# Latents turned piece by piece, scale and offset in quarters, split first transfers and a halved last tile in a fused encoder block

## The chip, the cores and the metric

The kernel runs on one core of a Trainium2 chip. The metric is device time in microseconds of one execution. The core has a matrix engine (TensorE, here PE, with the loading of weights shown apart as PEld), a vector engine (VectorE, DVE), a scalar engine (ScalarE, ACT), GpSimd (POOL) and a synchronising engine (SyncE, SP). Each has its own stream of instructions, which runs in order; SP, ACT and POOL also issue the transfers (DMAs) between the main memory and the on-chip memory.

## The reference

One layer of a streaming encoder with 256 tokens, width 2048, everything in float32. The residual stream `h` goes through four blocks, each closed by a LayerNorm over `ALPHA * h + block(h)`:

```python
h = LN(ALPHA*h + 0.5*swiglu_ffn(h, ffn1))             # 2048 -> 2 x 5504 -> 2048
proj = h @ w_in                                       # q, k, v of A; latents of B; gates
y_a = chunked_relbias_attention(qa, ka, va) @ w_o_a   # A: 16 heads of 64, relative bias
c_q  = rms_norm(q_lat, q_a_norm)                      # B: low-rank latents, 512 each
c_kv = rms_norm(c_kv, kv_a_norm)
y_b = mla(c_q @ w_q_b, c_kv @ w_kv_b, k_pe) @ w_o_b   # B: 16 heads of 128 + 64 rotary
h = LN(ALPHA*h + (sig(g_a)*y_a + sig(g_b)*y_b) @ w_out)
h = LN(ALPHA*h + cross_attention(h, LN(mem)))         # 4 heads of 512, 256 memory tokens
h = LN(ALPHA*h + 0.5*swiglu_ffn(h, ffn2))
```

A LayerNorm is `(x - mean) * rsqrt(var + eps) * g + b`, with a scale `g` and an offset `b` for each of the 2048 columns.

## The kernel before

**Numbers in two halves.** Each float32 operand of a large product is split into a rounded half `hi` and the rest `lo` (`split` at lines 234 and 235, `halves` for weights at lines 242 and 245). A product is then three passes: hi by hi, hi by lo, lo by hi. The cast to `hi` runs on ACT, the subtraction that gives `lo` on DVE.

**Weights.** All weights pass once through the core, in pieces of up to 128 x 2048 numbers (1 MB). A piece is fetched by SP into one of three `raw` tiles and split into one of two pairs of `hi` and `lo` tiles; `run` keeps the fetches about two pieces ahead of their use. Some pieces (`Sums`) are combined further on DVE (lines 189 and 191), which saves products.

**PSUM.** Two pools of four banks each, `mm` and `at`. A `pair_group` fills four tiles of 128 x 512 for two column groups and two token tiles; groups alternate between the pools. The attention parts use `at` for scores, transpositions and outputs.

**The order.** The program is a list of items (`add`, `weave`), each a function with the weights that it needs. A planner then orders the instructions of every engine by priority, by place in the list and by its own estimate of when an operand is ready. `prio(SOON)` and `prio(NEAR)` put the instructions of an item forward by 400 and 100 places, `prio(LATE)` puts them back by 400. The order that it finds is fixed; on the chip every engine follows it and waits where something is late.

**The start (`start`).** Twelve warm-up products (line 475) run on PE. Then eight steps `k`, each with two slices of the transposed input `xT` (0.25 MB, issued by ACT at line 483) and 1 MB of weights (SP, line 486; in halves for the first two steps); the slices and the weights are split, and 24 products of 512 columns follow (`mm_pair`, line 299).

**The mixer.** After the gates, the latents' product (`w_lat`) is formed. `lat_scale` normalises the two latents per token; `gb_apply(0)` multiplies the residual stream with the scale of the first LayerNorm and adds its offset, in four quarters of 512 columns: each loads a quarter of `g` and of `b` from POOL into two `w2` tiles (of five that all parts share) and runs two multiplications (line 444) and two additions (line 445) on DVE. Then come the shared rotary key (`kpe`, with swaps by SP at line 891), the query and key projections of the first two A heads (`a_proj(0)`, 64 products in two halves, lines 265 and 267), and `lat_turn`: both latents are transposed on PE (line 877, 16 transpositions of 128 x 128 into four `at` tiles), multiplied by their gains to give `hi` on ACT (line 881), and the rest `lo` on DVE (line 882). The A heads follow in pairs: projections, transpositions of the probabilities (line 774), scores (line 924), outputs (lines 965 and 966). The latents are first used by the rotary queries (line 255), after the A heads' projections. The 16 B heads (`b_scores`, `b_trans`, `b_proj`, `b_out`) come after; the softmax between scores and transposition runs on DVE and ACT (lines 762 to 769, 1039).

**The end.** The last product, `ffn2`'s second half over 19 row tiles, is done in groups of 4, 4, 4, 4 and 3 row tiles (`out_proj`, line 286). For the last 512 columns all groups of the first token tile run first and then those of the second (`skewed`), so that the first tile's LayerNorm and output run beside the second's products. After the last group, `finish` adds the 512 columns to `h` (line 701), takes their statistics (`bn_stats`, line 377), and `final_steps` aggregates them (line 382), forms the inverse root, applies scale and offset (lines 1320 and 1321) and writes the result.

## Time and profile before

| | us |
|---|---|
| median of three runs | 2495.51 (2494.61 to 2496.06) |
| the profiled execution | 2493.65 |
| its span in the profile | 2491.9 |

| engine | busy us | share of the span |
|---|---|---|
| PE | 2471.8 | 99% |
| PEld | 2082.8 | 84% |
| DVE | 2055.1 | 82% |
| ACT | 1332.9 | 53% |
| POOL | 28.8 | 1% |

The transfers move 490.03 MB, 197 GB/s on average. A row of the timeline gives start, duration, engine, line, operation, written tile `<-` read tiles, the shape, and in brackets the idle time of that engine before the row and what ended it. A row of the waits gives the waiting instruction, what it waited for, microseconds in all, times and the longest. In a row such as `x16` several instructions are merged; the duration is of all of them.

### The profile page before, as it was taken

The page shows a single profiled execution, that of the slowest core. Times are in us where ns is not written, and L with a number is a line of the kernel's source. Part 1 is how long each engine was busy: PE and PEld are TensorE (multiplying, and loading weights), DVE is VectorE, ACT ScalarE, POOL GpSimd, SP SyncE. Part 2 cuts the span into 40 slices and gives each one's busy share as a digit, 9 for nine tenths or more (in the row PEclk, how much of TensorE's full clock was granted, in tenths as well). Part 3 has the DMA queues.
Part 4 walks back from the last instruction along what each step waited for, and adds up shares of the span by engine and source line. Part 5 has one row for each costly group of instructions (what it writes and reads, how often), then busy time and mean ns, then how long its engine had stood idle before and what let it go on. Part 6 is the DMA issues. An engine that isn't in the chain of part 4 may idle for free.

```text
span 2491.9 us, 30464 instructions
## 1 busy us (share of the span) xinstructions
PE 2471.8 (99%) x11966; PEld 2082.8 (84%) x11966; DVE 2055.1 (82%) x2313; ACT 1332.9 (53%) x1798; POOL 28.8 (1%) x69
## 2 busy tenths in 40 slices
PE   9999999999999999999999999999999999999998
PEld 7888888889888888899888888898888888888886
DVE  6999889899778988676678798557888988898986
ACT  5555555555455555555445565545555555555552
POOL 0000000000000001000000000000000000000000
PEclk9999999999999999999999999999999999999999
DMA  7655555556645556543466557544555555655664
GB/s 255 240 191 208 188 201 209 203 186 204 236 160 203 210 203 226 199 153 119 168 221 219 186 175 247 189 167 148 205 204 186 203 186 203 210 198 201 206 211 141
DMA packets 72512, 490.03 MB, mean 197 GB/s; under 512 B 8368, under 2 KB 8752, under 8 KB 17200
## 3 DMA queue, kind: packets, MB, share of 16 engines
q1 hardware_dynamic: 66384, 467.11, 53.7%
q0 software_dynamic: 4256, 17.83, 2.2%
q10 hardware_dynamic: 1728, 3.15, 0.4%
q8 instruction: 93, 1.52, 0.2%
q14 instruction: 51, 0.42, 0.0%
HBM read 484.77 MB, written 2.10 MB: 195 GB/s over the span
## 4 chain that ended last, share of the span: by engine, by line
PE 95%; DVE 2%; DMA 1%; ACT 1%; issue 0%; SPq 0%; DVEq 0%; ACTq 0%; POOL 0%
PE mm L299 25%; PE at L299 25%; PE mm L353 10%; PE at L353 10%; PE mm L286 8%; PE mm L265 7%; PE mm L267 4%; PE mm L255 2%; PE at L924 1%; PE at L286 1%; DVE lo L245 1%; PE at L774 1%; DMA H<-xT 0%; PE at L1279 0%; PE at L404 0%; PE at L1255 0%
## 5 line engine op out<-in xcount | busy, mean ns | idle before, releaser
L242 ACT CAST hi<-raw 128x1024 fp32r<-128x1024 f32 (+1 forms) x848 | 801.8, 987 | 604.2 <-PE at L299 182.6
L245 DVE TENSOR_TENSOR lo<-raw,hi 128x2048 fp32r<-128x2048 f32 (+2 forms) x425 | 904.3, 2129 | 239.6 <-ACT hi L242 237.8
L299 PE MATMUL mm<-hi,T 128*128 128x512 f32 (+1 forms) x1280 | 298.4, 383 | 1.4 <-ACT hi L234 1.4
L242 ACT CAST X<-H 128x1024 fp32r<-128x1024 f32 (+1 forms) x162 | 164.9, 1034 | 216.7 <-DVE H L191 86.6
L299 PEld LDWEIGHTS mm<-hi,T 128*128 128x128 f32 x1280 | 238.0, 188 | 46.1 <-ACT hi L234 2.0
L299 PE MATMUL at<-hi,T 128*128 128x512 f32 x1072 | 257.0, 389 | 0.0
L245 DVE TENSOR_TENSOR X<-H,X 128x2048 fp32r<-128x2048 f32 (+1 forms) x81 | 182.3, 2251 | 67.7 <-ACT X L242 67.7
L299 PEld LDWEIGHTS at<-hi,T 128*128 128x128 f32 x1072 | 201.2, 188 | 41.9
L299 PE MATMUL mm<-lo,T 128*128 128x512 f32 (+1 forms) x640 | 153.8, 382 | 0.0
L299 PE MATMUL at<-hi,H 128*128 128x512 f32 x608 | 144.7, 390 | 0.9 <-DVE w L632 0.9
L299 PEld LDWEIGHTS mm<-lo,T 128*128 128x128 f32 x640 | 119.1, 188 | 21.8
L299 PEld LDWEIGHTS at<-hi,H 128*128 128x128 f32 x608 | 113.9, 188 | 24.7 <-DVE w L632 1.3
L299 PE MATMUL at<-lo,T 128*128 128x512 f32 x536 | 132.6, 389 | 0.0
L265 PE MATMUL mm<-T,hi 128*128 128x512 f32 x512 | 124.4, 394 | 0.0
L299 PEld LDWEIGHTS at<-lo,T 128*128 128x128 f32 x536 | 100.6, 188 | 20.9
L299 PE MATMUL mm<-hi,H 128*128 128x512 f32 x480 | 116.1, 392 | 0.0
L191 DVE TENSOR_TENSOR H<-H,raw 128x512 f32<-128x512 f32 (+1 forms) x162 | 109.5, 676 | 1.7
L265 PEld LDWEIGHTS mm<-T,hi 128*128 128x128 f32 x512 | 94.2, 189 | 19.3 <-issue 0.9
L299 PEld LDWEIGHTS mm<-hi,H 128*128 128x128 f32 x480 | 89.3, 188 | 18.2 <-DVE w L274 0.2
L189 DVE TENSOR_TENSOR H<-raw 128x1024 f32<-128x1024 f32 (+1 forms) x81 | 97.1, 1199 | 3.0 <-DMA raw<-ffn_w_in 1.7
L353 PE MATMUL mm<-X,X 128*128 128x512 f32 x348 | 95.9, 392 | 0.0
L242 ACT CAST X<-raw 128x1024 fp32r<-128x1024 f32 (+1 forms) x54 | 55.4, 1035 | 51.5 <-DVE raw L191 31.9
(321 smaller groups left out, 3913.9 us busy)
## 6 DMA issues: line engine op xcount, KB each, us to landing
raw<-ffn_w_in SPq DMA_DIRECT2D x150, 1024.0 KB, 4.8
raw<-ffn_w_out SPq DMA_DIRECT2D x66, 1024.0 KB, 4.8
raw<-w_gate SPq DMA_DIRECT2D x32, 1024.0 KB, 4.8
raw<-ffn_w_out_r SPq DMA_DIRECT2D x16, 1024.0 KB, 4.9
raw<-w_qk SPq DMA_DIRECT2D x16, 1024.0 KB, 4.8
raw<-w_o_b SPq DMA_DIRECT2D x16, 1024.0 KB, 4.8
raw<-w_out SPq DMA_DIRECT2D x16, 1024.0 KB, 4.8
raw<-w_xk SPq DMA_DIRECT2D x16, 1024.0 KB, 4.8
```

Source lines behind the costliest of these rows:

```text
L189: self.nc.vector.tensor_tensor(two[0], two[1], raw[:, :m].unsqueeze(1).to_broadcast([P, 2, m]), ALU.add)
L191: self.nc.vector.tensor_tensor(t[:, a * m:a * m + m], t[:, b * m:b * m + m], raw[:, a * m:a * m + m], ALU.add)
L242: self.nc.scalar.copy(hi[:, c:d], src[:, c:d])
L245: self.nc.vector.tensor_tensor(lo[:, :n], src, hi[:, :n].bitcast(F32), ALU.subtract)
L255: self.nc.tensor.matmul(ps, w[wi][:, cols[j]:cols[j] + P], x.at(xi, kt), start=(j + wi + xi == 0), stop=(j == n - 1 and wi == 1),)
L265: self.nc.tensor.matmul(ps, hi[kt], x.both(kt), start=(kt == 0), stop=False)
L267: self.last_mm = self.nc.tensor.matmul(ps[:, :S], lo[kt], x.at(0, kt), start=False, stop=(kt == n - 1))
L286: self.last_mm = self.nc.tensor.matmul(ps, x.at(xi, kt)[:, tt * P:(tt + 1) * P], w[wi][:, j * 512:(j + 1) * 512], start=(start and j + wi ...
L299: self.last_mm = self.nc.tensor.matmul(ps[tt, g][:, :n], x.at(xi, kt)[:, tt * P:(tt + 1) * P], w[wi][:, c:c + n], start=first and j + wi + ...
L353: self.last_mm = self.nc.tensor.matmul(bank[:, :m], a[xi], v[wi][:, c * m:(c + 1) * m], start=own and first and wi + xi == 0, stop=own and ...
L774: self.nc.tensor.transpose(ps[:, i * P:(i + 1) * P], s[:, c:c + P], self.ident)
L924: nc.tensor.matmul(ps[:, c0:c0 + nk], q[:, tt * P:(tt + 1) * P], k[:, :nk], start=(j == 0), stop=(j == len(parts) - 1))
```

## The change

It has four parts.

- **The latents** are turned in four pieces of four transpositions and one `at` tile each. Two stand behind the two halves of the second pair's projections (`a_proj(1)`), two behind those of the third (`a_proj(2)`), in place of one block behind `a_proj(0)`; their work on ACT and DVE gets the priority `NEAR`.
- **Scale and offset** of the first LayerNorm go in quarters, behind B heads 2, 5, 8 and 11, with the priority `LATE`, in place of all four behind `lat_scale`.
- **The start**: the first step's weights come in quarters and its two slices of x one by one; ACT issues the slices of the first three steps at once and SP those of the others, each two steps ahead of its weights' turn; the rounding of the first step's slices runs on DVE.
- **The end**: for the second token tile of the last 512 columns, the sum of the first four groups is added to `h` early, and the last group of three row tiles is formed as two tiles of 256 columns, each with its own addition and statistics; the last LayerNorm's statistics then have five parts.

```diff
-    def mm_tok(self, ps, tt, w, x, kts, start, stop):
+    def mm_tok(self, ps, tt, w, x, kts, start, stop, c=0, m=512):
...
-                        ps, x.at(xi, kt)[:, tt * P:(tt + 1) * P], w[wi][:, j * 512:(j + 1) * 512],
+                        ps, x.at(xi, kt)[:, tt * P:(tt + 1) * P], w[wi][:, j * 512 + c:j * 512 + c + m],
...
-    def gb_apply(self, i, h):
+    def gb_apply(self, i, h, qs=range(4)):
 
         nc = self.nc
-        for q in range(4):
+        for q in qs:
...
+        v = [xr[k // 4][:, k % 4 * 2:k % 4 * 2 + 2, :] for k in range(KT // 2)]
+
+        def x_load(q, k, step=2):
+            for i in range(0, 2, step):
+                q.dma_start(v[k][:, i:i + step, :], t["xT"][:, 2 * k + i:2 * k + i + step, :])
+        for k in range(3):
+            x_load(nc.scalar, k, 2 if k else 1)
         for k in range(KT // 2):
...
-            nc.scalar.dma_start(v, t["xT"][:, 2 * k:2 * k + 2, :])
-            for c in range(0, 2048, 1024 if k < 2 else 2048):
-                d = c + (1024 if k < 2 else 2048)
-                nc.sync.dma_start(raw[:, c:d], src[:, c:d])
-            self.split(v, xT.blk(0, 2 * k, 2), xT.blk(1, 2 * k, 2))
+            n = (512, 1024, 2048)[min(k, 2)]
+            for c in range(0, 2048, n):
+                nc.sync.dma_start(raw[:, c:c + n], src[:, c:c + n])
+            if 2 < k + 2 < KT // 2:
+                x_load(nc.sync, k + 2)
+            for i in range(0, 2, 1 if k == 0 else 2):
+                m = 1 if k == 0 else 2
+                hi, lo = (xT.blk(a, 2 * k + i, m) for a in (0, 1))
+                if k == 0:
+                    nc.vector.tensor_copy(hi, v[k][:, i:i + m, :])
+                    nc.vector.tensor_tensor(lo, v[k][:, i:i + m, :], hi.bitcast(F32), ALU.subtract)
+                else:
+                    self.split(v[k], hi, lo)
...
-                st[tt] = self.ln_begin()
+                st[tt] = self.ln_begin(5 if self.cut and tt else 4)
...
+                if cut and again and i == len(groups) - 1:
+                    for a in range(2):
+                        p = self.mm_tile()
+                        self.mm_tok(p[:, :S], 1, w, x(), grp, True, True, a * S, S)
+                        hs = h[1][:, n * 512 + a * S:n * 512 + a * S + S]
+                        with self.prio(SOON):
+                            nc.vector.tensor_tensor(hs, hs, p[:, :S], ALU.add)
+                            nc.vector.bn_stats(st[1][:, 3 + a, :], hs)
+                    return
                 for tt in tts:
...
+                    short = cut and again and i == len(groups) - 2
+                    self.mm_tok(ps[tt], tt, w, x(), grp, i == 0, short or i == len(groups) - 1)
+                    if short:
+                        hs = h[tt][:, n * 512:(n + 1) * 512]
+                        nc.vector.tensor_tensor(hs, hs, ps[tt], ALU.add)
...
-        def lat_turn():
-            self.c = self.act(["X0", "X1"])
-            for k in range(2):
-                for b in range(2):
-                    ps = self.at_tile()
+        def lat_turn(k, b):
+            def fn():
+                if k + b == 0:
+                    self.c = self.act(["X0", "X1"])
+                ps = self.at_tile()
+                for i in range(2):
...
+                    with self.prio(NEAR):
                         nc.scalar.mul(hi, p, gain)
                         nc.vector.scalar_tensor_tensor(lo, p, gain, hi.bitcast(F32), ALU.mult, ALU.subtract)
+            return fn
...
-        self.add(lambda: self.gb_apply(0, self.h), prio=LATE)
...
-        def a_proj(i):
+        def a_proj(i, side=()):
...
             for k in range(2):
                 self.add(one(k), t["w_qk"][i, k])
+                for f in side[k:k + 1]:
+                    self.add(f)
...
         a_proj(0)
-        self.add(lat_turn)
...
-                a_proj(i + 1)
+                a_proj(i + 1, [lat_turn(i, b) for b in range(2)] if i < 2 else ())
...
+            if h in (2, 5, 8, 11):
+                self.add(lambda q=h // 3: self.gb_apply(0, self.h, (q,)), held=int(h % 2 == 0), prio=LATE)
```

More of the change, by code (lines that the diff above doesn't have):

```diff
@@ L111, in __init__ @@
         self.chain = None
+        self.cut = False
     def name(self, s):
@@ L370, in rsqrt, with ln_begin @@
                 nc.vector.scalar_tensor_tensor(y, a, 1.5, y, ALU.add, ALU.mult)
[L373 to L374 removed]
+    def ln_begin(self, n=4):
+        return self.small.tile([P, 5, 6], F32, tag="bn", name=self.name("bn"))[:, :n, :]
     def ln_piece(self, st, h, n):
@@ L545, in ffn @@
                 self.add(late)
+                self.add(lambda: setattr(self, "cut", True))
             def out(hid=hid):
@@ L552, in out @@
                 if end:
-                    self.out_proj(tag + "_w_out_r", nf, x, False, st, steps, tags, 2)
+                    self.out_proj(tag + "_w_out_r", nf, x, False, st, steps, tags, 2, cut=tags is None)
                 else:
@@ L703, in finish, with out_proj @@
             if n == 0:
-                st[tt] = self.ln_begin()
+                st[tt] = self.ln_begin(5 if self.cut and tt else 4)
             self.ln_piece(st[tt], h[tt], n)
-    def out_proj(self, wname, nk, x, scale, st, steps=None, tags=None, n0=0, other=False):
+    def out_proj(self, wname, nk, x, scale, st, steps=None, tags=None, n0=0, other=False, cut=False):
         nc, t, h = self.nc, self.t, self.h
```

17 lines of the change are left out of this document (6 added, 11 removed).

## The prediction

> **What bounds the kernel now.** I read the page first, then the waits of the matmul engine, then the timelines of the places that the change touches.
>
> ```profile
> span 2491.9 us, 30464 instructions
> PE 2471.8 (99%) x11966; PEld 2082.8 (84%) x11966; DVE 2055.1 (82%) x2313; ACT 1332.9 (53%) x1798; POOL 28.8 (1%) x69
> PE 95%; DVE 2%; DMA 1%; ACT 1%; issue 0%; SPq 0%; DVEq 0%; ACTq 0%; POOL 0%
> ```
>
> TensorE (PE) is busy for 2471.8 of 2491.9 us and carries 95% of the chain that ended last. The change takes away no matmul, so all it can win lies in the 20.1 us in which PE stood still, plus stretches where PE ran slowly. The waits of PE say where these are; the rest, some 12 us, is the tail after the last matmul, and comes last below:
>
> ```profile
> PE at L877 <- DVE X L882: 3.6, 1, 3.6
> PE mm L299 <- ACT hi L234: 1.4, 2, 0.8
> PE at L475 <- DVE w L451: 1.1, 1, 1.1
> PE at L299 <- DVE w L632: 0.9, 1, 0.9
> PE at L404 <- DVE h L396: 0.5, 2, 0.3
> ```
>
> L877 is the turning of the latents, L299 with L234 the first group at the start. L632 and L404 are in code that the change leaves alone.
>
> **The turning of the latents (L877).** The timeline of all engines around the wait, and two stretches of the table by windows (length; busy time of PE, PEld, DVE, ACT, POOL; granted clock; DMA share; GB/s):
>
> ```profile
> 955.97 0.69 DVE L444 TENSOR_TENSOR h<-h,w 128x512 f32<-128x512 f32 x1 [1.84 <-DMA w<-gb]
> 958.38 2.08 PE L267 MATMUL mm<-T,lo 128*128 128x256 f32 x16
> 965.86 1.04 PE L877 MATMUL at<-ident,H 128*128 128x128 f32 x8
> 966.65 2.76 PE L265 MATMUL mm<-T,hi 128*128 128x512 f32 x11
> 967.12 2.29 DVE L245 TENSOR_TENSOR lo<-raw,hi 128x2048 fp32r<-128x2048 f32 x1
> 969.32 0.69 DVE L445 TENSOR_TENSOR h<-h,w 128x512 f32<-128x512 f32 x1
> 969.93 2.28 DVE L245 TENSOR_TENSOR lo<-raw,hi 128x2048 fp32r<-128x2048 f32 x1
> 972.46 2.91 DVE L882 SCALAR_TENSOR_TENSOR X<-at,vecs,X 128x256 fp32r<-128x256 f32 x7
> 972.99 0.44 PE L877 MATMUL at<-ident,H 128*128 128x128 f32 x2 [3.58 <-DVE X L882]
> 975.76 2.96 PE L267 MATMUL mm<-T,lo 128*128 128x256 f32 x16
> 965.86:984.21 18.35, 14.77 (x82) 12.79 (x80) 16.54 (x25) 8.04 (x15) 0.00 (x0) 0.91 0.50 171
> 1004.42:1009.99 5.57, 5.57 (x34) 4.92 (x33) 2.62 (x2) 2.27 (x4) 0.34 (x2) 1.00 0.37 104
> ```
>
> All sixteen transpositions of the turning are issued together. PE does eight of them, into two PSUM tiles, starts the next projection (L265), and then cannot go on: the eight others go out in twos, each pair behind an L882, which empties half a tile on VectorE (DVE). DVE has two splits of 2.29 us and an addition of the LayerNorm offset (L445) ahead of the first L882, 5.26 us by their rows.
>
> From 965.86 to 984.21 PE does the 16 transpositions and two halves of a query-key projection. One such half alone takes 5.57 us (last row). Eight transpositions take 966.65 - 965.86 = 0.8 us, so 16 take 1.6; cut into four places they need about 0.1 us more at each, an estimate. That makes 2 x 5.57 + 1.6 + 0.4 = 13.1 us against 18.35: 5.2 us are lost, the wait of 3.58 and 1.6 in which PE runs slowly behind it (the 16 matmuls of L267 take 2.96 us there and 2.08 at 958.38). The granted clock of 0.91 lies in the same stretch.
>
> The change puts one tile between projections, four times, some 5.6 us apart. Its drain (two multiplications on ScalarE, two L882, put forward by the priority) then has a projection's 5.57 us where before it had none. The last piece is the tight one: transpositions and scores follow it at once and ask for tiles within about 1 us. Bounds: a gain of all 5.2 us, or of 2.6 if half of the loss reappears there. I take 5.2, since the same tiles serve the later pairs of heads, five requests in a row, without a wait in the list above. Who needs the latents later? The rotary projections, some 80 us after; a piece that is two projections late costs nothing there.
>
> The Trainium skill, "TensorE: Matmul & The Clock Gate", Part 1, says that an idle window of about 3.4 us brings the clock to half. The trace agrees, with 0.91 over a stretch that holds 3.58 us of idleness. By that rule a wait cut to half would lose no clock either, which makes the second rival below 0.8 us better than I put it.
>
> **The start (L299 with L234).** Rows of the timeline, one of the chain, and two windows:
>
> ```profile
> 1.06 4.78 PE L475 MATMUL at<-w 128*128 128x128 f32 x24 [1.06 <-DVE w L451]
> 5.48 0.62 ACT L234 CAST T<-H 128x512 fp32r<-128x512 f32 x1 [2.79 <-DMA H<-xT]
> 6.67 3.99 PE L299 MATMUL mm<-hi,T 128*128 128x512 f32 x16 [0.83 <-ACT hi L234]
> 7.62 1.14 ACT L234 CAST hi<-raw 128x512 fp32r<-128x512 f32 x2 [0.48 <-DMA raw<-ffn_w_in]
> 13.23 0.62 ACT L234 CAST T<-H 128x512 fp32r<-128x512 f32 x1 [2.99 <-DMA H<-xT]
> 14.85 36.56 PE mm L299 x160
> 0.00:4.00 4.00, 2.94 (x14) 2.94 (x14) 0.17 (x1) 1.49 (x2) 1.69 (x10) 1.00 0.46 131
> 4.00:8.00 4.00, 3.17 (x18) 2.70 (x18) 1.87 (x3) 2.05 (x4) 0.00 (x0) 1.00 1.02 391
> ```
>
> The group has 192 matmuls of 36.56 / 160 = 0.228 us, so 43.9 us. It begins at 6.67 and ends at 14.85 + 36.56 = 51.41. The warm-up matmuls (L475) hold PE until 5.84, so it can't begin earlier; without gaps it would end at 49.7. The upper bound is therefore 1.7 us. The lower bound is set by the transfers, which already run at full rate: 131 GB/s make 0.52 MB by 4.0 us, and 0.39 MB come per us after that. The first weights arrived in halves of 0.5 MB beside 0.25 MB of x; the second half, with 1.5 MB moved by 6.5 us (two slices of x and the megabyte of weights), was seen at 7.62, so a landing is seen about 1.1 us after its bytes. In the new order the first matmul needs 0.13 MB of x and 0.25 MB of weights; with two queues sharing, that is 0.52 MB moved, 4.0 us, seen at 5.1, cast (half of 1.14) by 5.7: PE starts at 5.84. The second quarter needs 1.0 MB, so 5.3 + 1.1 + 0.6 = 7.0, where PE would want it at 6.3; the later quarters and the second block come in time, and the third slice of x, for which ScalarE sat 2.99 us at 13.23, is asked for at once rather than behind casts. So of 1.7 us some 0.5 are lost again: I take a gain of 1.2, bounds 0 and 1.7. That more and smaller transfers cost more on the SP queue I price at nothing: five slices of x now stand between the weight blocks there, 0.25 MB or 0.6 us each at 0.39 MB per us, and later blocks wait for their buffer, not for the queue. Uncovered, that is the 3 us that would undo the gain.
>
> **Scale and offset among the B heads.** Sixteen DVE adds and multiplications and eight POOL transfers leave the stretch from 952 to 990 us and go, a quarter at a time, behind heads 2, 5, 8 and 11. The price of one, the landings of the transfers of the scale (L440), the windows of the B heads, what DVE waited for there, and who waited for the last step of a softmax (L769):
>
> ```profile
> L444 DVE TENSOR_TENSOR h<-h,w x24: 675/684/694, 956.0 to 1824.0; 128x512 f32<-128x512 f32 x24
> DMA to landing us min/median/max: 3.3/4.1/9.9
> 1097.00:1160.00 63.00, 62.93 (x435) 58.46 (x435) 42.63 (x100) 34.49 (x86) 0.00 (x0) 1.00 0.38 132
> DVE sm_r L767 <- ACT w L765: 14.9, 13, 1.5
>   PEld at L774: 0.7, 2
> ```
>
> The 16 instructions are 16 x 0.684 = 10.9 us. DVE has 63.0 - 42.6 = 20.4 us free in this stretch, mostly the holes of about 1.1 us in which a softmax waits for its exponential (14.9 us in 13), and one addition fits such a hole. But PE is full, and two of the 16 softmaxes were finished only as PE came for them (0.7 us, last row): DVE work that slips in ahead delays PE. If every instruction had a chance of 2 in 16 to do so, it would cost 16 x 0.684 / 8 = 1.4 us; as the quarters have the lowest priority, I take half, 0.7. Below: nothing, as PE has no wait there to lose. Above: each quarter standing on the path with its four instructions (2.74 us) and the one wait for a transfer seen, 1.84 us (row of 955.97): 4 x 4.58 = 18.3 us. The space: of five w2 buffers three are in use by softmaxes and two go to a quarter, so nothing is left over, but nothing is short. On POOL's queue the eight transfers leave their place ahead of the A heads' biases, for which PE has no wait above, and come to where POOL is idle (0.00 in the window).
>
> **The tail.** From the timeline, with one row of half the width from elsewhere:
>
> ```profile
> 972.13 0.41 DVE L274 TENSOR_TENSOR w<-w,mm 128x256 f32<-128x256 f32 x1
> 2477.48 0.75 DVE L1321 SCALAR_TENSOR_TENSOR h<-h,y,T 128x512 f32<-128x512 f32 x1
> 2479.48 0.69 DVE L701 TENSOR_TENSOR h<-h,mm 128x512 f32<-128x512 f32 x1 [1.25 <-PE mm L286]
> 2480.20 0.69 DVE L377 BATCH_NORM_STATS2 bn<-h 128x6 f32<-128x512 f32 x1
> 2480.93 0.27 DVE L382 BATCH_NORM_AGGREGATE mv<-bn 128x2 f32<-128x24 f32 x1
> ```
>
> Behind the last matmul stand an addition and a statistic of 512 columns, 2480.93 - 2479.48 = 1.45 us. Halved, only 256 columns stay behind it: 0.41 for the addition and the same, estimated, for the statistic, with gaps about 0.85; gain 0.6. Nine matmuls of 512 columns (2.05 us) become 18 of 256 at 2.08 / 16 = 0.13 (L267 at 958.38), 2.3 us at most, so 0.1 to 0.3 go back. The early addition of 0.69 finds DVE free from 2478.23 on (a hole of 1.25 us), if it isn't ordered ahead of the other half's last steps. I take 0.4; bounds 0 and 0.6.
>
> **The sum.** -5.2 - 1.2 + 0.7 - 0.4 = -6.1 us. The profiled execution took 2493.65 us, 1.86 below the median of the three runs, 2495.51. Against the median I forecast 2489.4, that is -0.24%. What a measurement of this kernel can tell from no change is 0.2%, 5 us: the border lies at 2490.5.
>
> **The rivals.** First, slower: the quarters stand in the way of the B heads. Place: DVE between a head's scores and its transposition, price up to 4.58 us a quarter as above. It speaks for it that PE is full and that the trace has such a wait of 1.84 us; against it that of 24 instructions of L444 one waited. It cancels the other gains (6.8 us) from 1.7 us a quarter on, and decides for slower from 2.95 (11.8 / 4); at full price 2495.5 - 6.8 + 18.3 = 2507.0.
>
> On this the Trainium skill, "SBUF — State Buffer", section "SBUF: two separate sides", speaks against the change: while DVE runs certain instructions, POOL can't write the descriptors of its transfers. The landings of 3.3 to 9.9 us, for transfers of one size, fit that, but no row here shows a lock. As a mechanism of this kernel, in rows, a quarter would come late by one split, 2.29 us, and DVE wait for it: 4 x 2.29 = 9.2 us if all are bare, so 2495.5 - 6.8 + 9.2 = 2497.9, within 0.2% of before; it has a chance of 0.04, since no transfer of the later two such passes was waited for.
>
> Second, the wait of L877 is not gone but moved to the reuse of the last piece's tile: half of the 5.2 us returns, 2492.0, or a like loss arises among the B heads. For it: PE's order is fixed beforehand and DVE is busy 16.54 of 18.35 us there. Against: one tile at a time, and DVE is rid of the scale and offset.
>
> Third, the start isn't sooner because the transfers run at full rate either way: -4.9 us, 2490.6, at the border.
>
> **How the numbers follow.** The forecast has 0.62; the first rival 0.08, the late transfers 0.04, the second 0.14, the third 0.12. Half of the third lies on either side of the border: faster 0.62 + 0.06 = 0.68, same 0.04 + 0.14 + 0.06 = 0.24, slower 0.08. The likeliest alone spans 2486.5 (upper bounds of all gains, 7.5, and the waits at L632 and L404, 1.4, gone by a new order) to 2490.5. The range takes in the second and third rivals with 1.5 us of cost among the heads: 2486.5 to 2493.5.
>
> **What would show it.** The latents: no wait of PE at L877 and a clock of 1.00 from 960 to 1000 us; the first group ending near 50.2; no new wait of PE on L769 or on the scale and offset between 1080 and 1190; the aggregate of the last LayerNorm 1.0 to 1.2 us behind the last matmul. I am wrong if PE waits over 3 us among the B heads, or if the pieces of the latents wait for L882 as before.

## The result and the profile after

| | before | after |
|---|---|---|
| median, us | 2495.42 (2493.59 to 2498.33, 10 runs) | 2487.53 (2486.73 to 2493.1, 10 runs) |
| the profiled execution, us | 2493.65 | 2488.81 |
| its span, us | 2491.9 | 2487.0 |

The ratio is 0.9971, with an interval of 0.9961 to 0.998: 7.9 us or 0.29% faster. The two profiled executions are only 4.84 us apart, since the one of before lies 1.8 us below its median and the one of after 1.3 us above. A second profile of the changed kernel, taken later, has a span of 2484.8 us.

Lines of the code move with the change: 299 becomes 300, 265 and 267 become 266 and 268, 877 and 882 become 905 and 911, 444 and 445 become 445 and 446, 767 and 769 become 795 and 797, 774 becomes 802, 924 becomes 955. In the experiments that add lines further up, L878 and L890 stand for L877, L883 and L895 for L882. First the busy time of the engines, from the page of the changed kernel:

```profile
PE 2470.8 (99%) x11975; PEld 2083.1 (84%) x11975; DVE 2056.5 (83%) x2319; ACT 1332.8 (54%) x1797; POOL 28.7 (1%) x69
```

The busy time of PE is 1.0 us less, the span 4.9 us. Most of what went is idle time. All waits of PE that are listed (total, times, longest):

```profile
PE at L405 <- DVE h L397: 1.1, 2, 0.9
PE at L476 <- DVE w L452: 1.1, 1, 1.1
PE at L300 <- DVE w L647: 1.0, 1, 1.0
PE mm L354 <- DVE H L236: 0.6, 1, 0.6
PE at L802 <- DVE w L797: 0.5, 1, 0.5
```

The wait of the latents (3.6 us at L877 before) and that of the first group (1.4 us) are gone. L802 on L797, the transposition of the probabilities waiting for the last step of a softmax, is new in this list. The waits at L405 and L354, for DVE, are in code that the change leaves alone; they were 0.5 us and none before, and they differ from profile to profile.

The timeline of the changed kernel, by place: a half of a projection without a piece and the next one with the first piece in it (two pairs of transpositions), the scores and ACT's work behind the first pair of the last piece (990.52), the last quarter among the B heads, the tail.

```profile
965.34 3.82 PE L266 MATMUL mm<-T,hi 128*128 128x512 f32 x16
969.00 2.08 PE L268 MATMUL mm<-T,lo 128*128 128x256 f32 x16
970.91 0.38 PE L905 MATMUL at<-ident,H 128*128 128x128 f32 x2
973.97 0.44 PE L905 MATMUL at<-ident,H 128*128 128x128 f32 x2
975.18 2.06 PE L268 MATMUL mm<-T,lo 128*128 128x256 f32 x16
...
991.01 0.48 ACT L910 ACTIVATE X<-at,vecs 128x256 fp32r<-128x256 f32 x1
991.38 0.48 ACT L808 COPY w<-at 128x384 f32<-128x384 f32 x1
991.49 1.35 PE L955 MATMUL at<-w,w 64*128 64x128 f32 x8
...
1174.76 0.68 DVE L446 TENSOR_TENSOR h<-h,w 128x512 f32<-128x512 f32 x1
1176.77 0.33 PE L802 MATMUL at<-ident,w 128*128 128x128 f32 x1 [0.55 <-DVE w L797]
...
2470.16 5.03 PE L287 MATMUL mm<-X,H 128*128 128x512 f32 x30
2475.36 0.40 DVE L749 TENSOR_TENSOR h<-h,mm 128x256 f32<-128x256 f32 x1
2476.25 0.29 DVE L383 BATCH_NORM_AGGREGATE mv<-bn 128x2 f32<-128x30 f32 x1
```

Of the kernel before, the row that ends with its last matmul is this:

```profile
2474.52 4.92 PE L286 MATMUL mm<-X,H 128*128 128x512 f32 x21
```

So the last matmul ends at 2479.44 us before and at 2475.19 after. The aggregate started 1.49 us behind it (2480.93, in the prediction) and now starts 1.06 us behind it (2476.25).

The chain of the changed kernel at its start (start, duration, what):

```profile
1.06 5.49 PE at L476 x24
6.55 43.88 PE mm L300 x192
```

The first group now follows the warm-up products at once and ends at 6.55 + 43.88 = 50.43; before it was 51.41. The warm-up itself ended later in this profile (6.55 us for 5.84), so the group begins only 0.1 us sooner than before (6.67); the rest of the gain is that its 192 products leave no gaps. Two stretches of the table by windows (length; busy PE, PEld, DVE, ACT, POOL; clock; DMA share; GB/s), first before, then after:

```profile
966.00:980.00 14.00, 10.42 (x56) 8.96 (x54) 12.19 (x18) 6.14 (x13) 0.00 (x0) 0.88 0.49 175
```

```profile
966.00:980.00 14.00, 14.00 (x83) 11.48 (x82) 8.38 (x8) 5.78 (x9) 0.00 (x0) 1.00 0.50 180
1097.00:1160.00 63.00, 62.98 (x422) 57.76 (x421) 49.26 (x113) 35.04 (x85) 3.79 (x7) 1.00 0.45 144
```

Between 966 and 980 us PE has no idle time left, the clock is at 1.00, and DVE does 8.4 us of work where it did 12.2. That work is now among the B heads: 49.3 us of DVE in the 63 us where 42.6 stood before. What DVE waited for there:

```profile
DVE sm_r L795 <- ACT w L793: 10.2, 11, 1.4
DVE h L446 <- DMA w<-gb: 0.5, 1, 0.5
```

The holes in which DVE waits for exponentials shrank from 14.9 to 10.2 us: quarters lie in them. One does not: the last quarter's addition at 1174.76 stands just ahead of a softmax's last steps, and PE waits 0.55 us for these at 1176.77.

To put the time to places I took, in each kernel's trace, the start of the first matmul of a stage and the change of its distance from the stage before it (us, against the kernel before). "Latents" is the stretch from the first product of the shared key to the first rotary product, "B heads" from there to the first product behind the heads, which goes out between the last of them; "the end of the second product" is a point inside `ffn2`, near 1900 us. The kernels other than before and after are those of the experiments.

| kernel | end of first group | to LayerNorm 1 | to shared key | latents | B heads | to the end of the second product | to the last matmul | behind it |
|---|---|---|---|---|---|---|---|---|
| after | -1.0 | +0.5 | -0.1 | **-4.5** | +0.5 | +0.5 | -0.1 | -0.7 |
| after, second profile | -1.2 | -0.6 | 0.0 | **-4.6** | +0.3 | -0.3 | 0.0 | -0.7 |
| latents alone | +0.1 | +0.4 | 0.0 | **-0.8** | 0.0 | -0.1 | +1.3 | 0.0 |
| quarters alone | 0.0 | +0.6 | +0.1 | **-5.3** | +0.5 | -0.2 | -0.3 | 0.0 |
| start alone | -1.0 | -0.4 | 0.0 | +0.6 | 0.0 | -0.1 | -0.2 | -0.2 |
| end alone | -0.1 | -0.3 | 0.0 | 0.0 | 0.0 | +0.7 | +1.8 | -0.5 |
| quarters, start, end | -0.8 | -0.5 | 0.0 | **-5.3** | +0.3 | -0.3 | -0.3 | -0.7 |

Stages that no part touches (to LayerNorm 1, to the end of the second product, to the last matmul) vary by up to 1.8 us from profile to profile (+0.5 and +0.5 after come with the waits at L405 and L354 in the list above, +0.7 and +1.8 of the end alone with 2.0 us at L354 in its list), so no stage is read here below half a microsecond unless several kernels agree on it.

### The profile page after: what moved, and what is told of

It reads as the page before. It is cut to its first block, busy times and chain, and to the rows that moved or that the text cites. A ratio compares the mean times of both kernels' runs of the same rounds, so it can differ in the third digit from the quotient of the medians.

```text
span 2487.0 us, 30497 instructions
## 1 busy us (share of the span) xinstructions
PE 2470.8 (99%) x11975; PEld 2083.1 (84%) x11975; DVE 2056.5 (83%) x2319; ACT 1332.8 (54%) x1797; POOL 28.7 (1%) x69
## 3 DMA queue, kind: packets, MB, share of 16 engines
q10 hardware_dynamic: 1152, 1.84, 0.2%
## 4 chain that ended last, share of the span: by engine, by line
PE 96%; DVE 2%; DMA 1%; ACT 1%; issue 0%; DVEq 0%; ACTq 0%
PE mm L300 25%; PE at L300 25%; PE mm L354 10%; PE at L354 10%; PE mm L287 7%; PE mm L266 7%; PE mm L268 4%; PE mm L256 2%; PE at L955 1%; PE at L287 1%; PE at L802 1%; PE at L1311 0%; PE at L1287 0%; PE at L996 0%; DVE lo L246 0%; PE mm L705 0%
## 5 line engine op out<-in xcount | busy, mean ns | idle before, releaser
L354 PE MATMUL mm<-X,X 128*128 128x512 f32 x348 | 95.6, 391 | 0.6 <-DVE H L236 0.6
```

Source lines behind the costliest of these rows:

```text
L354: self.last_mm = self.nc.tensor.matmul(bank[:, :m], a[xi], v[wi][:, c * m:(c + 1) * m], start=own and first and wi + xi == 0, stop=own and ...
```

## Experiments

**The four parts, one at a time.** Each kernel is the one before with one part of the change.

*Latents in pieces alone.*

```diff
-        self.add(lat_turn)
...
-                a_proj(i + 1)
+                a_proj(i + 1, [lat_turn(i, b) for b in range(2)] if i < 2 else ())
```

> The kernel before with the latents alone in four pieces; scale and offset stay behind lat_scale. Theory (the pieces remove the wait at L877 by giving each tile a projection's time): PE no longer waits for L882, PE comes to the rotary projections (L255) 4 to 5 us sooner than in the kernel before, and the time falls by 4 to 5 us, ratio 0.998. Rival (the wait came from DVE being late with the scale and offset, L444 and L445): half of the wait stays or moves, the rotary projections come 1 to 2.5 us sooner at most, ratio 0.999 or more.

2494.94 us beside 2494.7, ratio 1.0 (0.9991 to 1.0008). PE's wait, the window and the timeline of this kernel:

```profile
PE at L877 <- DVE X L883: 3.4, 1, 3.4
966.00:980.00 14.00, 10.62 (x59) 8.64 (x58) 13.93 (x19) 4.34 (x7) 0.00 (x0) 1.00 0.62 215
973.86 1.29 DVE L444 TENSOR_TENSOR h<-h,w 128x512 f32<-128x512 f32 x2
976.27 2.28 DVE L245 TENSOR_TENSOR lo<-raw,hi 128x2048 fp32r<-128x2048 f32 x1
978.47 0.48 DVE L883 SCALAR_TENSOR_TENSOR X<-at,vecs,X 128x256 fp32r<-128x256 f32 x1
979.00 0.44 PE L877 MATMUL at<-ident,H 128*128 128x128 f32 x2 [3.38 <-DVE X L883]
```

The wait is there as before, now at the second pair of the first piece. DVE is full (13.93 of 14 us): the first drain (L883) stands behind multiplications (973.86) and additions of the quarters and a split (976.27). A piece is one tile, and its second pair goes out 0.05 us behind the drain of its first pair (978.47 + 0.48 to 979.00): the second half of a tile waits for the drain of the first half. So the wait lies inside a tile, and one tile at a time does not help when the engine that empties it comes 6 us after the transposition (972.28 to 978.47). Read in this way, the eight transpositions that the block sends at once are the first halves of its four tiles. The theory put first fails. The stage gains 0.8 us in this profile, since the clock stays at 1.00; the medians show no gain.

*Scale and offset in quarters alone.*

```diff
-        self.add(lambda: self.gb_apply(0, self.h), prio=LATE)
...
+            if h in (2, 5, 8, 11):
+                self.add(lambda q=h // 3: self.gb_apply(0, self.h, (q,)), held=int(h % 2 == 0), prio=LATE)
```

> The kernel before with scale and offset alone moved in quarters among the B heads; the latents stay one block behind a_proj(0). Theory: the block still waits for its L882 behind the two splits of 2.29 us on DVE, so PE still waits 2.5 to 3.5 us at L877, the rotary projections come at most 1.5 us sooner; the B heads cost 0 to 1 us; ratio 0.9995 to 1.0005. Rival (DVE was late through the scale and offset): the wait falls under 1 us, the rotary projections come 3 to 5 us sooner, ratio 0.998.

2488.17 us beside 2494.7, ratio 0.997 (0.9959 to 0.9982). The window and the first drains of the latents, which are turned in one block here as before:

```profile
966.00:980.00 14.00, 14.00 (x92) 12.31 (x93) 8.69 (x14) 8.83 (x16) 0.00 (x0) 1.00 0.55 194
969.44 3.37 DVE L882 SCALAR_TENSOR_TENSOR X<-at,vecs,X 128x256 fp32r<-128x256 f32 x8
```

No wait at L877, PE full, the clock at 1.00. The whole gain of the latents, 5.3 us, comes from this part; the rival of the expectation holds.

*The start alone.* The diff of `start` as shown with the change, and nothing else.

```diff
-            for c in range(0, 2048, 1024 if k < 2 else 2048):
...
+            n = (512, 1024, 2048)[min(k, 2)]
...
+            if 2 < k + 2 < KT // 2:
+                x_load(nc.sync, k + 2)
```

> The kernel before with the new first transfers alone. Theory: the first group ends 1.0 us sooner (near 50.4 instead of 51.4 us), all later work of PE is shifted by as much, the time falls by 1 us, ratio 0.9996. Rival (the first microsecond is lost again at the next wait): the first group ends sooner but PE comes to the first LayerNorm's transpositions (L404) at the same time as before, ratio 1.000.

2493.2 us beside 2494.7, ratio 0.9993 (0.9984 to 1.0002). The time alone doesn't tell it from nothing; the first group ends 1.0 us sooner in this trace (50.2 by the stages for 51.2 before), as it does in every kernel that has this part and the twelve warm-up products (0.8 to 1.3 us). The latents' wait is untouched:

```profile
PE at L890 <- DVE X L895: 4.0, 1, 4.0
```

*The end alone.* The diff of `out_proj` as shown with the change.

```diff
+                if cut and again and i == len(groups) - 1:
+                    for a in range(2):
+                        p = self.mm_tile()
...
+                            nc.vector.bn_stats(st[1][:, 3 + a, :], hs)
```

> The kernel before with the last tile halved alone. Theory: PE ends 0.2 us later, the aggregate of the last LayerNorm stands 1.06 us behind PE's end instead of 1.49, and the time falls by 0.2 to 0.4 us, ratio 0.9999, not to be told from 1 by time, only in the profile. Rival (the early addition is ordered ahead of the other half's last steps and delays them): the aggregate comes as late as before or later.

2494.45 us beside 2494.7, ratio 0.9996 (0.9987 to 1.0005). The aggregate starts 1.07 us behind the end of the last matmul, and 1.06 or 1.07 in every kernel with this part, for 1.49 in those without it. The 1.8 us that this profile loses ahead of the last matmul are not in the others; they are waits at L354, which the part does not touch.

Added up, the four medians against before make +0.24 - 6.5 - 1.5 - 0.25 = -8.0 us; the whole change made -7.9. The parts do not help or hinder each other beyond what these runs resolve.

**All but the pieces.** The changed kernel with the latents turned in one block as before; run beside the changed kernel itself.

```diff
-                a_proj(i + 1, [lat_turn(i, b) for b in range(2)] if i < 2 else ())
+                a_proj(i + 1)
...
         a_proj(0)
+        self.add(lat_turn)
```

> The changed kernel with the latents left as one block behind a_proj(0), so quarters, start and tail without the pieces. Theory now (the quarters' move alone takes the wait away, and the pieces cost PE some 0.8 us, since their transpositions go out in twos between other matmuls): no wait at L877, PE comes to the rotary projections about 0.8 us sooner than in the changed kernel, measured from the shared key's product on, and the time is 0.5 to 1 us under the changed kernel's, ratio to the kernel before 0.9967. Rival (the pieces carry a part of the gain in this company): a wait at L877 of over 1 us and a time above the changed kernel's.

> The changed kernel once more beside the others of this call. Both theories: ratio 0.9971 as before, within 0.001; the rotary projections 4 to 5 us sooner than in the kernel before.

Without the pieces 2486.5 us, ratio 0.9967 (0.9955 to 0.9979); the changed kernel beside it 2486.87, ratio 0.9969 (0.9957 to 0.9981). The times are the same; the latents' stretch gains 5.3 us without the pieces and 4.5 to 4.6 with them, in three profiles each. So the pieces cost 0.8 us there.

**Why the quarters were in the way.** They put three things ahead of the first drain: instructions on DVE, DVE's waits for the transfers, and a place in its queue.

*The first quarter stays, the other three move.*

```diff
-        self.add(lambda: self.gb_apply(0, self.h), prio=LATE)
+        self.add(lambda: self.gb_apply(0, self.h, (0,)), prio=LATE)
...
+            if h in (5, 8, 11):
+                self.add(lambda q=h // 3: self.gb_apply(0, self.h, (q,)), held=int(h % 2 == 0), prio=LATE)
```

> The kernel before with the quarters of heads 5, 8 and 11 moved and the first quarter left behind lat_scale; the latents one block. Theory (VectorE's instructions and its wait ahead of L882 add up): four instructions of 0.65 us at spacing and a wait of 1.8 us come back, of which about 3 us fall into holes of VectorE that the quarters-alone run has, so PE waits 0.5 to 2 us at L877. Rival (the wait for the first quarter's transfer alone makes the lateness, which shifts the swaps of the rotary key and all that follows): PE waits 3 us or more, as in the kernel before.

2489.27 us beside 2494.54, ratio 0.9978 (0.997 to 0.9987). PE's wait and two rows of DVE:

```profile
PE at L877 <- DVE X L882: 0.9, 1, 0.9
956.66 0.69 DVE L444 TENSOR_TENSOR h<-h,w 128x512 f32<-128x512 f32 x1 [2.49 <-DMA w<-gb]
969.78 3.37 DVE L882 SCALAR_TENSOR_TENSOR X<-at,vecs,X 128x256 fp32r<-128x256 f32 x8
```

DVE still waits 2.5 us for the first transfer, and PE's wait falls from 3.6 to 0.9 us all the same. That one wait is not the cause by itself.

*The priority put back by 3000 places instead of 400.*

```diff
-        self.add(lambda: self.gb_apply(0, self.h), prio=LATE)
+        self.add(lambda: self.gb_apply(0, self.h), prio=-3000)
```

> The kernel before with one number changed: the priority of scale and offset behind lat_scale is put back by 3000 places instead of 400. Theory (what counts is that VectorE's order has scale and offset ahead of the latents' L882, not where they stand in the list): the wait at L877 falls under 1 us and PE comes from the shared key's product to the rotary projections 3.5 to 5.3 us sooner, ratio 0.997 to 0.9985. Rival (VectorE has not the room for them among the A heads): the wait turns up as waits of PE in the A heads, the same stretch gains under 2 us, ratio 0.999 or more.

2494.55 us beside 2495.14, ratio 1.0 (0.9991 to 1.0009).

```profile
PE at L877 <- DVE X L882: 4.3, 1, 4.3
972.67 2.59 DVE L882 SCALAR_TENSOR_TENSOR X<-at,vecs,X 128x256 fp32r<-128x256 f32 x6
```

The order on DVE stays nearly what it was: the planner gives DVE whatever is ready by its estimate, however low its priority, and on the chip the instruction then stands there. So this run does not show whether DVE would have room for the quarters among the A heads in another order. It shows that priority does not move them, and a place in the list does.

*All sixteen instructions, two transfers instead of eight.*

```diff
-            g, b = self.w2(), self.w2()
-            nc.gpsimd.dma_start(g, self.t["gb"][i, 0:1, cs].to_broadcast([P, 512]))
-            nc.gpsimd.dma_start(b, self.t["gb"][i, 1:2, cs].to_broadcast([P, 512]))
+            if i > 0 or q == 0:
+                g, b = self.w2(), self.w2()
+                nc.gpsimd.dma_start(g, self.t["gb"][i, 0:1, cs].to_broadcast([P, 512]))
+                nc.gpsimd.dma_start(b, self.t["gb"][i, 1:2, cs].to_broadcast([P, 512]))
```

> The kernel before, in which all four quarters of the first LayerNorm use the scale and the offset of the first: two transfers instead of eight, the same sixteen additions and multiplications in the same order on DVE. (The values of three quarters are therefore those of another column; this leaves out six transfers and nothing else.) Open is what of the quarters delays the turning of the latents: their instructions on DVE, or their transfers, which crowd the swap of the shared key (in the kernel before DVE waits 1.7 us for it, with all the quarters moved away not at all). Theory A, the instructions: seven of them still stand ahead of the first L882, the wait of PE at L877 stays at 3.0 us or more and the stretch from the shared key to the first rotary product gains less than 1.0 us. Theory B, the transfers: the swap comes 1.7 us sooner and with it everything behind it in DVE's queue; the wait of PE falls to between 1.5 and 2.3 us, the clock stays at 1.00, and the stretch gains 1.9 + 1.6 = 3.5 us (2.5 to 4.3); time about 2491.5 beside 2495. If the wait falls below 1.0 us, the instructions have no part in it at all.

2492.04 us beside 2495.4, ratio 0.999 (0.9981 to 0.9999). The stages put only 0.3 us of this on the latents, and 1.0 us on the stage ahead of the last matmul, which varies by that much. Its lines are one higher: L445 is the multiplication, L878 the transposition.

```profile
PE at L878 <- DVE X L883: 3.3, 1, 3.3
957.36 0.69 DVE L445 TENSOR_TENSOR h<-h,w 128x512 f32<-128x512 f32 x1 [3.41 <-DMA w<-gb]
972.03 2.90 DVE L883 SCALAR_TENSOR_TENSOR X<-at,vecs,X 128x256 fp32r<-128x256 f32 x7
966.00:980.00 14.00, 10.66 (x56) 9.19 (x55) 12.21 (x17) 6.97 (x14) 0.00 (x0) 0.88 0.43 153
```

By the expected numbers the instructions are right and the transfers wrong: the wait is 3.3 us and the stage gains 0.3. The wait for the swap of the shared key (1.7 us before) did go, but the first transfer was waited for 3.4 us instead of 1.84, so DVE's waits for transfers in sum hardly fell (3.4 us for 3.55), and the test did not take them away as meant.

The four kernels with the block of latents and the kernel before can be set side by side. From the first product of the shared key (949.87 in the kernel with the quarters moved, 949.23, 949.00, 949.18 and 948.66 in the others, in the order of the table) to the first drain:

| kernel | first drain after | plus its 0.48, less PE's arrival at 20.2 | PE's wait |
|---|---|---|---|
| quarters moved | 19.6 | -0.1 | none |
| first quarter stays | 20.55 | 0.8 | 0.9 |
| two transfers | 23.0 | 3.3 | 3.3 |
| before | 23.3 | 3.6 | 3.6 |
| put back by 3000 | 24.0 | 4.3 | 4.3 |

PE's arrival is the end of its eight transpositions and eleven products, 966.65 + 2.76 - 949.18 = 20.2 in the kernel before. The wait is in every case what the first drain is late. What DVE did between the shared key and the first drain shows why it is late; the first row is the kernel before, the second the one with the quarters moved:

```profile
949.18:972.46 23.28, 20.23 (x116) 17.51 (x114) 19.59 (x36) 12.47 (x24) 5.05 (x12) 1.00 0.81 272
949.87:969.44 19.57, 19.57 (x114) 17.32 (x113) 15.93 (x30) 12.36 (x24) 0.68 (x4) 1.00 0.68 240
```

With the quarters moved DVE works 3.7 us less, but it stands still nearly as long: 3.2 us for casts on ACT, where before it stood 3.55 us for two transfers. So DVE had 3.2 us to spare, and the quarters put 3.7 us of work and 3.55 us of waiting on top: 3.7 + 3.55 - 3.2 = 4.0, and the drain came 3.7 us later. The same sum gives 1.2 us for "first quarter stays" (work 1.9, wait 2.5), 3.7 for "two transfers" (3.5 and 3.4) and 4.7 for "put back by 3000" (3.7 and 4.2); measured are 1.0, 3.5 and 4.4. So the two causes are of like size, and by this sum either one alone would have made the drain late by 0.5 us or less, an estimate. A kernel in which the transfers land in time, which would show that, was not run.

**The quarters put forward among the B heads** instead of back.

```diff
-                self.add(lambda q=h // 3: self.gb_apply(0, self.h, (q,)), held=int(h % 2 == 0), prio=LATE)
+                self.add(lambda q=h // 3: self.gb_apply(0, self.h, (q,)), held=int(h % 2 == 0), prio=SOON)
```

> The changed kernel with the quarters among the B heads put forward (SOON) instead of back (LATE). Theory (a quarter that stands ahead of a softmax on VectorE delays PE): PE waits among the B heads rise from under 1 us to 3 to 18 us, time 2 to 15 us above the changed kernel's, ratio 0.998 to 1.003. Rival (VectorE has the room anyway, the priority is without effect): waits under 1 us, time as the changed kernel's.

2488.04 us, ratio 0.9972 (0.9961 to 0.9982); the changed kernel beside it took 2486.87.

```profile
PE at L802 <- DVE w L797: 1.2, 1, 1.2
```

The B heads lose 1.0 us instead of 0.3 to 0.5, and the one wait of a transposition grows from 0.5 to 1.2 us. That lies between the two expectations (waits of 3 us or more, or under 1). Even with the quarters ahead of the softmaxes the price stays far below the 18.3 us that were the upper bound.

**Fewer warm-up products.** With the new order of transfers the first group could begin before the warm-up ends. The kernel without the pieces, with 8 warm-up products for 12.

```diff
-WARM = 12
+WARM = 8
```

> Quarters, start and tail without the pieces (as e7), with 8 warm-up products instead of 12. Theory (the first products wait for the warm-ups, which end near 6.2 us while x and weights are cast by 5.6): the first group begins 0.3 to 0.6 us sooner and ends as much sooner, time 2486. Rival (the transfers set the pace of the first quarters): the first group begins sooner but ends at the same 50.2 to 50.4 us, time as e7; or the array is slower for want of warm-up and the group ends 1 us later.

2488.84 us, ratio 0.9976 (0.9966 to 0.9986). The first row of the group, with 12 warm-up products and then with 8, and for the latter two windows of equal length:

```profile
6.20 4.50 PE L300 MATMUL mm<-hi,T 128*128 128x512 f32 x16
```

```profile
5.57 6.08 PE L300 MATMUL mm<-hi,T 128*128 128x512 f32 x16 [0.72 <-ACT hi L235]
6.00:10.20 4.20, 4.20 (x11) 3.24 (x11) 3.44 (x7) 2.84 (x5) 0.00 (x0) 1.00 1.01 386
10.30:14.50 4.20, 4.20 (x20) 3.42 (x19) 3.52 (x4) 2.09 (x3) 0.00 (x0) 1.00 1.05 420
```

PE begins 0.6 us sooner, but its first sixteen products take 6.1 us instead of 4.5 and the group ends at 51.4, 1.0 us later than with 12. Until 10.2 us PE does 11 products in 4.2 us, after that 20, and the trace's record of the clock begins at that moment, 10.21 us (with 12 warm-up products at 6.63 in the profile shown). The start of the data does not bound the first group any more; the moment at which the clock rises does. The medians lie 2.3 us apart, of which the group explains 1.0; the rest lies in stages that vary.

**The pieces in one place, later.** The changed kernel with its four pieces together behind the second half of the second pair's projection.

```diff
-                a_proj(i + 1, [lat_turn(i, b) for b in range(2)] if i < 2 else ())
+                a_proj(i + 1, [lambda: None, lambda: [lat_turn(k, b)() for k in range(2) for b in range(2)]] if i == 0 else ())
```

> The changed kernel with its four pieces one behind the other behind the second half of a_proj(1) instead of spread over four places. Theory (the 0.8 us that the pieces cost come from the spreading, transpositions in twos between other products): from the shared key's product to the rotary projections PE takes 0.4 to 0.9 us less than in the changed kernel. Rival (the cost comes from the later place, where scores and softmax need VectorE as well): the stretch takes as long as in the changed kernel or longer, with a wait at L877.

2486.39 us, ratio 0.9966 (0.9953 to 0.9979); span 2483.6 us. The latents' stretch gains 5.2 us, as with the block in its old place.

```profile
975.23 1.03 PE L905 MATMUL at<-ident,H 128*128 128x128 f32 x8
989.92 0.86 ACT L808 COPY w<-at 128x384 f32<-128x384 f32 x2
990.14 0.93 PE L955 MATMUL at<-w,w 64*128 64x128 f32 x8
```

So the place costs nothing, the spreading does, in two shares. In the changed kernel the sixteen products of 512 columns with the first piece in them take 975.18 - 970.91 = 4.27 us, against 969.00 - 965.34 = 3.66 without: 0.3 for each of the two pairs of transpositions, where eight in a row take 0.8 here (975.23 to 976.02), 0.2 a pair. In a block eight go out in a row and eight in four pairs, in pieces all go out in pairs: four pairs more at 0.1, so 0.4 us. The other 0.4 is the scores behind the last piece's first pair, which take 1.35 us (991.49, above) where they take 0.93 here. The pool `at` has four tiles, and there five are asked for in a row: the piece's, two for transpositions, two for scores; the piece's is held until its second pair is drained. In the trace the second head's scores go out at 991.91, 0.05 us behind ACT's first copy (991.38 + 0.48), which empties a transposition's tile and itself stands behind the piece's multiplication (L910). Here the copies have no such multiplication ahead of them. This last step is read from the rows; no kernel tests it. This kernel and the one without pieces are the fastest measured; over the changed kernel they are ahead by some 0.4 us, which the intervals don't separate.

## Why the prediction was right, and where it was not

The time, the range and the direction held: 2489.4 forecast, 2487.5 measured. The working held less well.

- **The latents, -5.2 us.** The size was right (-4.5 with the pieces, -5.3 without), the cause was wrong. The step that failed is the one that gave the gain to the pieces: "Its drain ... then has a projection's 5.57 us where before it had none". The pieces alone leave a wait of 3.4 us. I had listed the splits and the addition that stood ahead of the first L882, and yet treated the move of the quarters as a cost only. What removes the wait is that the quarters' instructions and transfers leave DVE's queue: -5.3 us. The pieces by themselves cost 0.8 us: 0.4 for their cutting, as I had put, and 0.4 at the last piece, which I had called the tight one and then priced at nothing.
- **"I take 5.2, since the same tiles serve the later pairs of heads"** told nothing about the drain: in the kernel before not the tile was scarce, the engine that empties it was late. The eight transpositions at once went "into two PSUM tiles" in the prediction; the pieces show that they are the first halves of four, since in a piece too the second pair waits for the drain of the first, so that time between the tiles takes nothing off this wait. A tile is scarce only behind the last piece, for 0.4 us.
- **The slow PE behind the wait.** The 1.6 us belong to the clock, as supposed: with the pieces alone the window shows a clock of 1.00 at a wait of 3.38 us and no slow products behind it, and the stage gains 0.8 although the wait stays (1.6 of the clock and 0.2 of a shorter wait, less what the pieces cost). That gain is luck, as the record of the clock shows. The Trainium skill, "TensorE: Matmul & The Clock Gate", Part 1, puts the window at about 3.4 us and calls it free-running. The trace agrees: in each of the five profiles with slow products (before, start alone, end alone, put back by 3000, two transfers) the recorded clock is 0.50 for 3.41 us, and the time from the start of the record to there is a whole number of such windows (969.385 us before, 284 times 3.4133). What decides is how long PE is idle within one of these windows, and not how long it waits at one time. Two windows of the kernel with two transfers, then two with the pieces alone:

```profile
970.53:973.94 3.41, 1.38 (x9) 1.28 (x10) 3.41 (x7) 0.90 (x2) 0.00 (x0) 1.00 0.85 334
973.94:977.36 3.42, 3.42 (x15) 3.18 (x14) 2.67 (x6) 2.76 (x5) 0.00 (x0) 0.50 0.58 242
```

```profile
973.70:977.12 3.42, 1.92 (x9) 1.26 (x7) 3.42 (x6) 0.00 (x0) 0.00 (x0) 1.00 0.96 376
977.12:980.53 3.41, 1.53 (x10) 1.39 (x11) 3.41 (x6) 0.78 (x2) 0.00 (x0) 1.00 0.28 58
```

In the first pair 2.0 us of a wait of 3.3 us fall into one window, PE is busy for 1.38 us of it, and the next window has half the clock. In the second pair the border at 977.12 cuts a wait of 3.38 us in two, PE is busy for 1.92 and 1.53 us of the two windows, and the clock stays. In the five profiles PE was busy for 0.04 to 1.38 us of the window ahead of the slow one; where between 1.38 and 1.53 us the limit lies is not measured.

- **The start, -1.2 us.** Right: -1.0 to -1.2 in the profiles of the change; the group ends at 50.4, where 50.2 was forecast. The third rival falls. That the warm-up holds PE until 5.84 us was not a fixed bound: it ended at 6.55 in the first profile of the change, whose clock record begins at 7.13 us, where that of before begins at 4.94.
- **The quarters among the B heads, +0.7 us.** Right: 0.3 to 0.5 us, and 1.0 with the quarters put ahead. The first rival (18.3 us) falls: holes of the exponentials take the work, as argued. The sign "no new wait of PE" did not hold: there is one, of 0.55 us, behind a quarter's addition, which is what the 0.7 was meant for. The late transfers of its second form (9.2 us) were not seen either: the one wait of DVE for such a transfer among the B heads is 0.5 us. The Trainium skill, "SBUF — State Buffer", "SBUF: two separate sides", has POOL held off from writing its descriptors while DVE runs certain instructions; no row here shows that. The same section of the Trainium skill says that `tensor_tensor` was not seen to stall a transfer, and the split that the prediction took for the price of the lock is one (TENSOR_TENSOR in the rows).
- **The tail, -0.4 us.** Right: the aggregate starts 1.06 instead of 1.49 us behind the last matmul (I had said 1.0 to 1.2), 0.43 sooner, and the eighteen narrow products, 0.12 us apart, take PE 0.1 us longer than nine wide ones, so -0.3. The -0.7 of the last stage counts from the start of the last matmul, which is itself 0.1 us shorter, and holds 0.2 us that the start alone shows too, without this part.
- **The second rival** (the wait moves to the reuse of a tile, 2492.0) comes near the kernel with the pieces alone, whose wait moved into the first piece, though between the halves of one tile and not to the reuse of the last. In the whole change it does not come about, since the quarters are gone from there; what is left of it is the 0.4 us behind the last piece.
- **Against the median** the sum of -6.1 became -7.9. The stages of the second profile of the change (2486.58 us) make -7.1: the touched ones -1.2, -4.6, +0.3 and -0.7, so -6.2, and 0.9 in stages that the change leaves alone. That rest is explained only in part: PE waits 0.3 us less at L405 than before. The two profiles of the changed kernel differ there by more (0.5 and -0.6 in one stage).

Still open: why the second half of a tile waits for the drain of the first, what the drain would do with the quarters' instructions in place and their transfers in time, and whether the quarters would fit among the A heads in another order on DVE.

## What to carry to other kernels

When PE waits for an engine that empties a tile, list everything that stands ahead of the emptying instruction in that engine's queue, and ask of each part of a change whether it takes something out of that list: that, and not the shape of the waiting work, decided here. Then set the work and the waits on that list against what the engine has to spare: 3.7 and 3.55 us met 3.2 us of slack, and only what was over delayed PE. A low priority does not keep work off the path if the planner puts it into any hole it sees; moving it to another place in the list does. And a change with four parts that comes out as forecast has not confirmed the reasons: here the part credited with the gain costs 0.8 us and the part priced as a cost brings it.

## What was not expected of the hardware

With 8 warm-up products instead of 12, sixteen products of 512 columns took 6.08 us instead of 4.50, though the clock column shows 1.00 in these windows. The column says nothing there: the record of the clock begins only at 10.21 us in that trace, and a stretch without a record is printed as 1.00. The products change pace at that very moment, from 0.43 to 0.23 us from start to start. In the thirteen profiles with 12 warm-up products the record begins between 4.1 and 7.1 us. And the landing of the same first transfer of the scale moved between runs of nearly the same program: DVE waited 1.84 and 2.64 us for it where eight such transfers are issued, 2.49 and 3.41 where two are.
